# A decoder trunk's first modulation: four parts of 256 features in place of two of 512, with products of two k blocks between them

## The chip, the cores and the metric

The kernel runs on one core of a Trainium2 chip. The metric is the device time of one execution in microseconds (us); before the change it is 2655.22 us, the median of three runs (2654.45 to 2656.13). The engines are PE (TensorE: matrix products and transposes; its weight loads are shown apart as PEld), DVE (VectorE), ACT (ScalarE), POOL (GpSimd) and SP (SyncE, which only issues DMAs here). Each engine takes its instructions strictly in the order in which the program lists them, and waits on semaphores for what other engines or DMAs have to deliver first.

## The reference

Two layers of a decoder on a sequence of 1024 tokens with 1024 features. Every sub-layer is modulated by a vector `c`: a shift, a scale and a gate, each of 1024 features, computed from `c` by one large matrix. The change touches only the first sub-layer's shift and scale, and the first half of what follows them, the columns of `v` in the gated mixer:

```
def ada_mod(c, w, b):
    m = jax.nn.silu(c) @ w + b
    shift, scale, gate = jnp.split(m, 3, axis=-1)
    return shift[:, None, :], scale[:, None, :], 1.0 + gate[:, None, :]

...
    shift, scale, gate = ada_mod(c, ada_w[i, 0], ada_b[i, 0])
    h = x * (1.0 + scale) + shift
...
    uv = jax.nn.gelu(h @ w_in + b_in)
    u, v = jnp.split(uv, 2, axis=-1)
```

All is float32. The kernel gets that precision from products of reduced-precision pairs: an operand is split into a high part (a cast) and a low part (the remainder), and a product is three matmuls: high by high, high by low, low by high.

## The kernel before

The tokens are eight tiles of 128 rows, the features eight k blocks of 128. The first phase is `mixer_a` (L494). It computes, for the first 512 columns of `v`, `v = h @ w_in`, tile by tile and k block by k block, with one PSUM bank for each tile (`psv`).

What must happen first is the modulation. `silu_c` holds silu(c) as eight columns, one for each k block. `ada_rows` (L595) loads one k block of the matrix, 128 rows by 2 x 512 features (shift and scale; 512 KB, rows of 2 KB). DVE multiplies it by its column and adds it to `adaacc` (L619, L621, L645, L647, one instruction of 1024 elements for each block; below, a *step*). When all eight are in, eight small matmuls with a column of ones (`psa_sum`, L606) sum over the partitions and leave shift and scale as columns; `columns` (L598) adds the bias. This is done twice: `mods_first` (L612) for features 0 to 511 (k blocks 0 to 3 of h), `mods_second` (L637) for features 512 to 1023.

`build_hT` (L235), called through `rows_of` (L546), makes h for some tiles and one k block: PE transposes the tiles of x into a PSUM bank (`pst`, L241), ACT applies scale and shift into `h` (L246) and casts the high part (L250), DVE forms the remainder (L251; `hT` in DVE's rows). `h` has two buffers and so have the PSUM banks that `pst` and `psa` share. `v_sum` (L522) issues the products (three for a tile and k block). `v_high` and `v_low` (L510, L518) split 1024 elements of weights, two k blocks, on ACT and DVE.

The order is written out by hand. `in_turn` (L551) is a generator that runs through a list of (tiles, k block): the h of an item is built two items ahead of its products. Between its stops the code places the other work: `mods_second` hands out turns after its steps 1, 2, 4, 6 and 7. `tc.keep_in_program_order` pins an instruction to its place in the order of its engine. While the first modulation is being loaded, PE runs matmuls on ready data without use of the result (`warm_up`, L587): 8 and 13, and 4 more later. All loads are issued on SP's one queue, in the order of the code, and at most eight are under way at a time: the ninth waits for the first to land.

Of the kernel before, what the change touches and what calls it, by code (L numbers as in the profile page):

```python
# [35 lines left out]
def trunk(ctx: ExitStack, tc: tile.TileContext, x, c, ada_w, ada_b, ln_g, ln_b, a_w_in, a_b_in,  # L36
# [83 lines left out]
    def ada_steps(j, order, raw_bufs=2):  # L120
# [4 lines left out]
        for part, h in order:  # L125
# [3 lines left out]
            def step(k, part=part, h=h, box=box, w0=w0):  # L129
                nm = f"{j}_{part}_{h}"  # L130
                raw = ada_p.tile([P, HALF], F32, name=f"adaw_{nm}_{k}", tag="adaw", bufs=raw_bufs)
                nc.sync.dma_start(raw[:], ada_w[i, s, k * P : (k + 1) * P, w0 : w0 + HALF])
                if k == 0:
                    acc = box["acc"] = ada_p.tile([P, HALF], F32, name=f"adaacc_{nm}", tag=f"adaacc{part % 2}")
                    ins = V.tensor_scalar(acc[:], raw[:], silu_c[:, 0:1], None, ALU.mult)
                else:
                    acc = box["acc"]
                    ins = V.scalar_tensor_tensor(acc[:], raw[:], silu_c[:, k : k + 1], acc[:], ALU.mult, ALU.add)  # L138
                tc.keep_in_program_order(ins)
# [354 lines left out]
    def mixer_a():  # L494
        nonlocal ada_p, vec
        with ExitStack() as ph:
# [13 lines left out]
            def v_high(c, kp):  # L510
                raw = vz[:, kp, :] if kp > 1 else wts.tile([P, D], F32, name=f"winv_{c}_{kp}_raw", tag="raw", bufs=2)[:]
                src = a_w_in[0, 2 * kp * P : 2 * (kp + 1) * P, D + c * HALF : D + (c + 1) * HALF]
                nc.sync.dma_start(raw.rearrange("p (k n) -> p k n", n=HALF), src.rearrange("(k p) n -> p k n", p=P))
                hi, lo = units[c, kp] = tuple(wts.tile([P, D], F32R, name=f"winv_{c}_{kp}_{m}", tag=f"w{m}")[:] for m in ("hi", "lo"))
                tc.keep_in_program_order(A.copy(hi, raw))
                parts_of[c, kp] = lo, raw, hi

            def v_low(c, kp):  # L518
                lo, raw, hi = parts_of.pop((c, kp))
                tc.keep_in_program_order(V.tensor_tensor(lo, raw, hi, op=ALU.subtract))  # L520
# [16 lines left out]
            def v_act(c, i):  # L537
                z = vz[:, i, c * HALF : (c + 1) * HALF]
                A.activation(z, z, AF.Gelu_apprx_tanh)
                V.bn_stats(st_v[:, i, c, :], z)  # L540
# [10 lines left out]
            def in_turn(*runs, begin=False):  # L551

                todo = [(i0, n, k) for i0, n, ks in runs for k in ks]
# [6 lines left out]
                for m in range(2):  # L560
                    rows(m)
                    yield
                for m, (i0, n, k) in enumerate(todo):
                    parts = [(i0, TERMS)]
                    if begin and m < 2:
                        parts = [[(0, TERMS[:1]), (0, TERMS[2:])], [(2, TERMS[:1]), (0, TERMS[1:2]), (2, TERMS[2:]), (2, TERMS[1:2])]][m]
                    for i1, terms in parts:
                        for i in range(i1, i1 + n):
                            v_sum(0, i, k, begin, terms)
# [3 lines left out]
            def x_cols(h, tiles):  # L573
                w = slice(h * HALF, (h + 1) * HALF)
                for i in tiles:
                    nc.sync.dma_start(xs[i][:, w], x_in[i * P : (i + 1) * P, w])

            first_ks, last_ks = range(KD // 2), range(KD // 2, KD)
            with tc.tile_pool(name="ada0", bufs=2, reuse_waits="tile") as ada0:
                warm = hT[1][0][:, KD - 1, :]  # L580
                acc = vec.tile([P, 2, HALF], F32, name="adaacc", tag="gate")
# [11 lines left out]
                xs += [work.tile([P, D], F32, name=f"x0_{i}", tag="res", bufs=3) for i in range(4, 7)]  # L593

                def ada_rows(h, k, raw):  # L595
                    nc.sync.dma_start(raw, ada_w[0, 0, k * P : (k + 1) * P, 0 : 2 * D].rearrange("p (t n) -> p t n", t=2)[:, :, h * HALF : (h + 1) * HALF])

                def columns(h, p):  # L598
                    for part in (1, 0):
                        src = p[:, 8 * part : 8 * part + 8].rearrange("p (k t) -> p k t", t=2)[:, :, 0]  # L600
                        bias = cols_b[:, 8 * part + 4 * h : 8 * part + 4 * h + 4]
                        res = ada[0][("add", "mul")[part], h] = cst.tile([P, 4], F32, name=f"ada_0_{part}_{h}")
                        ins = V.scalar_tensor_tensor(res[:], src, float(part), bias, ALU.add, ALU.add)
                        tc.keep_in_program_order(ins)

                def psa_sum(p, part, src, col):  # L606
                    for q in range(4):
                        tc.keep_in_program_order(T.matmul(
                            p[:, 8 * part + 2 * q : 8 * part + 2 * q + 1], src[:, part, q * P : (q + 1) * P], col,
                            start=True, stop=True))  # L610

                def mods_first():  # L612
                    p = bank("tr", "psa_0")
                    for k in range(KD):
                        raw = vz[:, k, :].rearrange("p (t n) -> p t n", t=2)
                        ada_rows(0, k, raw)
                        col = silu_c[:, k : k + 1]
                        if k == 0:
                            V.tensor_scalar(acc[:], raw, col, None, ALU.mult)  # L619
                        elif k < KD - 1:  # L620
                            tc.keep_in_program_order(V.scalar_tensor_tensor(acc[:], raw, col, acc[:], ALU.mult, ALU.add))  # L621
                        else:
                            for part in (1, 0):
                                tc.keep_in_program_order(V.scalar_tensor_tensor(acc[:, part, :], raw[:, part, :], col, acc[:, part, :], ALU.mult, ALU.add))
                        if k == 2:
                            tc.keep_in_program_order(A.copy(warm, raw[:, 0, :]))
                            warm_up(8)
                            pt = bank("tr", "rows_bt")
                            tc.keep_in_program_order(T.transpose(pt[:, 0:P], rows_b[:], ident[:]))
                            warm_up(13)  # L630
                        elif k == 5:
                            tc.keep_in_program_order(V.tensor_copy(cols_b, pt[:, 0:64]))
                    for part in (1, 0):
                        psa_sum(p, part, acc, one[:])
                    columns(0, p)

                def mods_second(between):  # L637
                    for k in range(KD):
                        if k < 6:
                            raw = ada0.tile([P, 2, HALF], F32, name=f"adaw_0_1_{k}", tag="adaw", bufs=6)[:]  # L640
                        else:
                            raw = vz[:, k - 6, :].rearrange("p (t n) -> p t n", t=2)
                        ada_rows(1, k, raw)
                        if k == 0:
                            ins = V.tensor_scalar(acc[:], raw, silu_c[:, 0:1], None, ALU.mult)  # L645
                        else:
                            ins = V.scalar_tensor_tensor(acc[:], raw, silu_c[:, k : k + 1], acc[:], ALU.mult, ALU.add)  # L647
                        tc.keep_in_program_order(ins)
                        for f in between.get(k, ()):
                            f()  # L650
                    p = bank("tr", "psa_1")
                    for part in (1, 0):
                        psa_sum(p, part, acc, one[:])
                    columns(1, p)
# [3 lines left out]
                mods_first()  # L658
                v_high(0, 0)
                x_cols(0, range(4))  # L660
                turns = in_turn((0, 2, (0,)), (2, 2, (0,)), (0, 2, (1,)), (2, 2, (1,)), (0, 4, (2, 3)), (4, 2, first_ks), begin=True)
                v_low(0, 0)
                next(turns)
                warm_up(4)
                next(turns)
                next(turns)
                next(turns)
                v_high(0, 1)
                v_low(0, 1)
                x_cols(0, (4, 5))  # L670
                next(turns)
                mods_second({k: [lambda: next(turns)] for k in (1, 2, 4, 6, 7)})
                x_cols(1, range(4))
                v_high(0, 2)
                next(turns)
                v_low(0, 2)
                rest = in_turn((0, 4, last_ks), (4, 2, last_ks), (6, 2, range(KD)))
                next(rest)
                run(turns)
                v_high(0, 3)  # L680
                v_low(0, 3)
                x_cols(1, (4, 5))
                nc.sync.dma_start(vbias[:], a_b_in[0, D : 2 * D].partition_broadcast(P))
# [1396 lines left out]
```

## Time and profile before

| What | us |
|---|---|
| median of three runs | 2655.22 |
| the profiled execution | 2655.62 |
| its span, from the first instruction to the last | 2653.9 |
| ACT in 40 to 60 us | 14.23 busy of 20 |
| DVE in 40 to 60 us | 11.60 busy of 20 |
| PE in 40 to 60 us | 19.98 busy of 20 |
| PE in 80 to 100 us | 19.64 busy of 20 |

An engine's busy time is the time during which it executes something; waits and DMA issues are not in it. Where an engine is busy all of the time, its own work sets the pace; where another has gaps, the question is whether anyone waits for it. Times in rows of the timeline are microseconds from the start of the span.

### The profile page before, as it was taken

The page shows a single profiled execution, that of the slowest core. Times are in us where ns is not written, and L with a number is a line of the kernel's source. Part 1 is how long each engine was busy: PE and PEld are TensorE (multiplying, and loading weights), DVE is VectorE, ACT ScalarE, POOL GpSimd, SP SyncE. Part 2 cuts the span into 40 slices and gives each one's busy share as a digit, 9 for nine tenths or more (in the row PEclk, how much of TensorE's full clock was granted, in tenths as well). Part 3 has the DMA queues.
Part 4 walks back from the last instruction along what each step waited for, and adds up shares of the span by engine and source line. Part 5 has one row for each costly group of instructions (what it writes and reads, how often), then busy time and mean ns, then how long its engine had stood idle before and what let it go on. Part 6 is the DMA issues. An engine that isn't in the chain of part 4 may idle for free.

```text
span 2653.9 us, 36921 instructions
## 1 busy us (share of the span) xinstructions
PE 2631.0 (99%) x13144; PEld 2179.2 (82%) x13144; DVE 1979.9 (75%) x3558; ACT 1397.1 (53%) x2639; POOL 104.8 (4%) x190
## 2 busy tenths in 40 slices
PE   8999999999999999999999999999999999999998
PEld 6888888888888888888888888888888888888887
DVE  6886898886988787655557777777669965677887
ACT  5454475555444554333436666666657655554432
POOL 0000000000000001111110000000010000000000
PEclk9999999999999999999999999999999999999999
DMA  8543367778867546565565554555783654495562
GB/s 298 187 120 119 127 199 237 240 233 287 315 212 248 186 151 230 192 205 195 175 188 159 151 148 129 141 143 144 233 222 120 211 186 152 151 320 190 180 208 86
DMA packets 341554, 505.35 MB, mean 190 GB/s; under 512 B 58092, under 2 KB 175444, under 8 KB 341368
## 3 DMA queue, kind: packets, MB, share of 16 engines
q1 hardware_dynamic: 324936, 444.22, 53.2%
q0 software_dynamic: 16432, 58.76, 6.2%
q8 instruction: 103, 1.69, 0.3%
q14 instruction: 83, 0.68, 0.1%
HBM read 365.95 MB, written 136.95 MB: 189 GB/s over the span
## 4 chain that ended last, share of the span: by engine, by line
PE 70%; issue 21%; DVE 4%; POOL 2%; DMA 1%; ACT 1%; POOLq 0%; SPq 0%; DVEq 0%; ACTq 0%
PE psua L987 13%; PE psd L1154 12%; PE psk L1600 7%; PE psuc L987 7%; PE psq L1600 6%; PE psd_wout L432 3%; PE psub L987 3%; PE psv L528 3%; PE pv L1773 3%; PE psu L774 3%; PE sc L1693 3%; PE pT L1746 1%; POOL v L1475 1%; PE psoa L1977 1%; POOL qk L1470 1%
## 5 line engine op out<-in xcount | busy, mean ns | idle before, releaser
L987 PE MATMUL psua<-right,left 128*128 128x512 f32 x1536 | 362.9, 390 | 0.1
L1154 PE MATMUL psd<-rhi,lhi 128*128 128x512 f32 x880 | 343.3, 390 | 0.0
L1154 PE MATMUL psd<-rhi,llo 128*128 128x512 f32 x880 | 342.5, 389 | 0.0
L1154 PE MATMUL psd<-rlo,lhi 128*128 128x512 f32 x880 | 342.4, 389 | 0.0
L987 PEld LDWEIGHTS psua<-right,left 128*128 128x128 f32 x1536 | 287.4, 188 | 61.1 <-DVE left L112 0.7
L1715 ACT ACTIVATE p<-p,stat 128x128 f32<-128x128 f32 (+1 forms) x384 | 168.7, 441 | 95.4 <-DVE stat L1713 93.4
L1154 PEld LDWEIGHTS psd<-rhi,lhi 128*128 128x128 f32 x880 | 165.3, 188 | 34.8 <-ACT part L1018 0.9
L1154 PEld LDWEIGHTS psd<-rhi,llo 128*128 128x128 f32 x880 | 165.3, 188 | 34.2
L1154 PEld LDWEIGHTS psd<-rlo,lhi 128*128 128x128 f32 x880 | 165.3, 188 | 33.8
L987 PE MATMUL psuc<-right,left 128*128 128x512 f32 x768 | 186.5, 390 | 0.0
L987 PEld LDWEIGHTS psuc<-right,left 128*128 128x128 f32 x768 | 143.8, 188 | 30.2 <-DVE right L112 0.6
L112 DVE TENSOR_TENSOR pTlo<-pT,pThi 128x512 fp32r<-128x512 f32 (+1 forms) x160 | 99.3, 621 | 76.1 <-ACT pThi L111 75.0
L112 DVE TENSOR_TENSOR left<-ws,left 128x512 fp32r<-128x512 f32 x128 | 88.0, 689 | 81.9 <-ACT left L111 80.1
L112 DVE TENSOR_TENSOR llo<-lraw,lhi 128x1024 fp32r<-128x1024 f32 x112 | 136.2, 1218 | 2.3 <-ACT lhi L111 2.3
L1600 PE MATMUL psk<-form_L,wqk_hi 128*128 128x512 f32 x384 | 127.3, 413 | 1.0 <-DVE qlo L112 1.0
L1600 PE MATMUL psq<-form_L,wqk_hi 128*128 128x512 f32 x384 | 126.7, 411 | 0.0
L111 ACT CAST lhi<-lraw 128x1024 fp32r<-128x1024 f32 x112 | 117.0, 1047 | 11.6 <-PE psd L1154 6.7
L1498 PE MATMUL psv<-vrhi,form_S 128*128 128x512 f32 x384 | 120.0, 391 | 1.4 <-DVE vpart L1464 0.9
L111 ACT CAST left<-ws 128x512 fp32r<-128x512 f32 x128 | 79.2, 620 | 80.0 <-DVE ws L911 69.4
L111 ACT CAST pThi<-pT 128x512 fp32r<-128x512 f32 (+1 forms) x160 | 84.7, 530 | 61.8 <-PE pT L1746 44.9
L1713 DVE CUSTOM_DVE_ANT_0 p<-sc,bias 128x128 f32<-128x128 f32 (+1 forms) x384 | 113.5, 345 | 4.5 <-PE sc L1693 3.3
L138 DVE SCALAR_TENSOR_TENSOR adaacc<-adaw,silu_c,adaacc 128x512 f32<-128x512 f32 x140 | 104.5, 747 | 6.6 <-DMA adaw<-in_ada_w_dram 5.6
(369 smaller groups left out, 6079.8 us busy)
## 6 DMA issues: line engine op xcount, KB each, us to landing
lraw<-forms SPq DMA_DIRECT2D x112, 512.0 KB
adaw<-in_ada_w_dram SPq DMA_DIRECT2D x160, 256.0 KB
up<-in_mlp_w_up_dram SPq DMA_DIRECT2D x64, 512.0 KB
forms<-s SPq DMA_DIRECT2D x128, 256.0 KB
rraw<-in_mlp_w_down_dram SPq DMA_DIRECT2D x64, 512.0 KB
forms<-part SPq DMA_DIRECT2D x96, 256.0 KB
v<-vs POOLq DMA_DIRECT2D x48, 512.0 KB, 3.6
vraw<-in_b_w_qkv_dram SPq DMA_DIRECT2D x42, 512.0 KB
```

The lines of the kernel that those rows point to most:

```text
L111: first = A.copy(hi, src) if hi_engine is A else hi_engine.tensor_copy(hi, src)
L112: return first, lo_engine.tensor_tensor(lo, src, hi, op=ALU.subtract)
L138: ins = V.scalar_tensor_tensor(acc[:], raw[:], silu_c[:, k : k + 1], acc[:], ALU.mult, ALU.add)
L432: T.matmul(p[:], stat[a][:, k, o : o + P], u[b][:, w], start=n == 0, stop=n == count - 1)
L528: ins = T.matmul(sums[i][:], hT[half][a_][:, k, o : o + P], units[c, k // 2][b_][:, n : n + HALF], start=k + a_ + b_ == 0, stop=k == KD - ...
L774: T.matmul(p[:], wu[a_][:, k * P : (k + 1) * P], hT[half][b_][:, k, :], start=k + a_ + b_ == 0, stop=k == KD - 1 and a_ == 1)
L987: T.matmul(acc, w[:, a, k, :], right[p][:, b, k, :], start=p in (1, 2, 5) and k + a + b == 0, stop=k == 3 and a == 1, skip_group_check=True)
L1154: ins = T.matmul(sums[kind, m][:, w], l[a][:, k, m * P : (m + 1) * P], r[b][:, k, w], start=p in (1, 5, 2, 3) and kp + k + a + b == 0 or b ...
L1498: T.matmul(acc, rows[:, m * P : (m + 1) * P], cols_, start=p in (1, 2, 5) and kp + k + a + b == 0, stop=kp == 1 and k == 1 and a == 1, ski ...
L1600: T.matmul(p[:], wu[a][:, k * P : (k + 1) * P], h_op(k, half, b), start=k + c_ == 0, stop=k == KD - 1 and c_ == 2)
L1713: V.tensor_tensor_reduce(out=pr, in0=banks[e][:, sl], in1=st["bias"][:, width - w :], scale=-0.125, scalar=3e38, op0=ALU.add, op1=ALU.min, ...
L1715: A.activation(pr, pr, AF.Exp, bias=nm, scale=-1.0, accum_out=l)
```

## The change

The first sub-layer's modulation is computed in four parts of 256 features (a part gives two k blocks of h) in place of two of 512. A load is 128 rows by 2 x 256 features (256 KB, rows of 1 KB), and a step has 512 elements. Part 0's first product is made by ACT into a tile of its own (`adaacc_a`), and the small matmuls add it to the rest. `adaacc` has two halves, used in turn. After part 0, the products of k blocks 0 and 1 for tiles 0 to 5 run; after part 1 those of k blocks 2 and 3, and so on (`quarter`, `middle`). The weights of `v` are split in halves, one k block at a time, and the first one is loaded in halves too. The tiles' order within a k block is changed, as is the order in which finished sums are taken out (`v_add`, `v_act`). There are 8 + 1 + 4 warming matmuls in place of 8 + 13 + 4. All of these loads are pinned in SP's order, and so are the weights of the gate that is computed later.

```diff
+            def v_high(kp, n):
+                w = slice(n * HALF, (n + 1) * HALF)
+                tc.keep_in_program_order(A.copy(units[0, kp][0][:, w], parts_of[kp][:, w]))
...
+                def mods_step(u, k):
+                    a, raw, col = acc[:, u % 2], raws.pop((u, k)), silu_c[:, k : k + 1]
+                    if k == (u == 0):
+                        ins = V.tensor_scalar(a, raw, col, None, ALU.mult)
+                    else:
+                        ins = V.scalar_tensor_tensor(a, raw, col, a, ALU.mult, ALU.add)
+                    tc.keep_in_program_order(ins)
...
+                def mods_end(u):
+                    p = bank("tr", f"psa_{u}")
+                    psa_sum(p, acc[:, u % 2])
+                    columns(u, p)
...
+                first = in_turn([(0, 2, 0), (2, 2, 0), (0, 2, 1), (2, 2, 1), (4, 2, 0), (4, 2, 1)], begun=TERMS[1:2])
...
+                mods_step(1, 0)
...
+                next(first)
+                mods_step(1, 1)
+                mods_step(1, 2)
+                next(first)
+                for k in (3, 4, 5):
+                    mods_step(1, k)
+                next(first)
+                mods_step(1, 6)
+                mods_step(1, 7)
+                v_high(1, 0)
+                mods_end(1)
+
+                def quarter(u, last):
+                    turns = in_turn([(i0, n, k) for k in (2 * u, 2 * u + 1) for i0, n in ((4, 2), (0, 4))], late=(0,))
+                    next(turns)
+                    v_high(u, 1)
+                    v_low(u, 0)
+                    for _ in last:
+                        pass
+                    next(turns)
+                    v_low(u, 1)
+                    next(turns)
+                    return turns
...
+                def middle(u, turns):
+                    next(turns)
+                    mods_step(u, 0)
+                    mods_step(u, 1)
+                    next(turns)
+                    for k in range(2, KD):
+                        mods_step(u, k)
+                    v_high(u, 0)
+                    mods_end(u)
+
+                middle(2, second)
+                third = quarter(2, second)
...
+                middle(3, third)
...
+                fourth = quarter(3, third)
-                mods_second({k: [lambda: next(turns)] for k in (1, 2, 4, 6, 7)})
```

How this stands on the engines is shown by the order of their instructions. A row gives the line, the operation, out<-in by the program's names and the shape. `adaacc` is the running sum, `psa` its small matmuls, `pst_0_3` the transposes of tiles 0 to 3 (`pst_4_...`: tiles 4 and 5) for k block 3, `h_0_3` the same after scale and shift, `hT_0_1` and `hT_1_1` the remainders of tiles 0 to 3 and of tiles 4 to 7.

DVE before, from the second modulation's fourth step to the columns that it gives:

```order
L647 SCALAR_TENSOR_TENSOR adaacc<-adaw_1_3_330,silu_c,adaacc 128x1024
L647 SCALAR_TENSOR_TENSOR adaacc<-adaw_1_4_333,silu_c,adaacc 128x1024
L251 TENSOR_TENSOR hT_1_1_139<-h_4_0_339,hT_1_0_138 128x256
L647 SCALAR_TENSOR_TENSOR adaacc<-adaw_1_5_355,silu_c,adaacc 128x1024
L647 SCALAR_TENSOR_TENSOR adaacc<-vz,silu_c,adaacc 128x1024
L251 TENSOR_TENSOR hT_1_1_139<-h_4_1_363,hT_1_0_138 128x256
L647 SCALAR_TENSOR_TENSOR adaacc<-vz,silu_c,adaacc 128x1024
L251 TENSOR_TENSOR hT_1_1_139<-h_4_2_380,hT_1_0_138 128x256
L603 SCALAR_TENSOR_TENSOR ada_1_1_399<-psa_390,cols_c 128x4
L603 SCALAR_TENSOR_TENSOR ada_0_1_401<-psa_390,cols_c 128x4
L251 TENSOR_TENSOR hT_1_1_139<-h_4_3_414,hT_1_0_138 128x256
```

DVE now, at the place of the third part of the four:

```order
L253 TENSOR_TENSOR hT_1_1_139<-h_4_3_396,hT_1_0_138 128x256
L625 TENSOR_SCALAR adaacc<-adaw_2_0_274,silu_c 128x512
L627 SCALAR_TENSOR_TENSOR adaacc<-adaw_2_0_274,silu_c,adaacc 128x512
L253 TENSOR_TENSOR hT_0_1_137<-h_0_3_419,hT_0_0_136 128x512
L627 SCALAR_TENSOR_TENSOR adaacc<-adaw_2_2_277,silu_c,adaacc 128x512 x2
L627 SCALAR_TENSOR_TENSOR adaacc<-adaw_2_4_280,silu_c,adaacc 128x512 x2
L627 SCALAR_TENSOR_TENSOR adaacc<-adaw_2_6_283,silu_c,adaacc 128x512 x2
L643 SCALAR_TENSOR_TENSOR ada_1_1_160<-psa_436,cols_c 128x2
L643 SCALAR_TENSOR_TENSOR ada_0_1_159<-psa_436,cols_c 128x2
L253 TENSOR_TENSOR hT_1_1_139<-h_4_4_446,hT_1_0_138 128x256
```

Before, one or two steps of 1024 stood between two remainders; now two steps of 512 stand before the remainder of `h_0_3`, and six behind it, with the columns of the part right after them.

PE before, around the second modulation's small matmuls:

```order
L528 MATMUL psv_4_367<-winv_0_hi,hT_1_0_138 128x512
L528 MATMUL psv_4_367<-winv_0_lo,hT_1_0_138 128x512
L528 MATMUL psv_4_367<-winv_0_hi,hT_1_1_139 128x512
L528 MATMUL psv_5_371<-winv_0_hi,hT_1_0_138 128x512
L528 MATMUL psv_5_371<-winv_0_lo,hT_1_0_138 128x512
L528 MATMUL psv_5_371<-winv_0_hi,hT_1_1_139 128x512
L608 MATMUL psa_390<-one,adaacc 128x1 x8
L241 MATMUL pst_4_3_411<-ident,x_4_153 128x128
L241 MATMUL pst_4_3_411<-ident,x_5_154 128x128
L528 MATMUL psv_4_367<-winv_1_hi,hT_1_0_138 128x512
L528 MATMUL psv_4_367<-winv_1_lo,hT_1_0_138 128x512
```

PE now, around the third part's:

```order
L243 MATMUL pst_0_3_414<-ident,x_0_150 128x128
L243 MATMUL pst_0_3_414<-ident,x_1_151 128x128
L243 MATMUL pst_0_3_414<-ident,x_2_152 128x128
L243 MATMUL pst_0_3_414<-ident,x_3_153 128x128
L538 MATMUL psv_4_327<-winv_1_hi,hT_1_0_138 128x512
L538 MATMUL psv_4_327<-winv_1_lo,hT_1_0_138 128x512
L538 MATMUL psv_4_327<-winv_1_hi,hT_1_1_139 128x512
L538 MATMUL psv_5_331<-winv_1_hi,hT_1_0_138 128x512
L538 MATMUL psv_5_331<-winv_1_lo,hT_1_0_138 128x512
L538 MATMUL psv_5_331<-winv_1_hi,hT_1_1_139 128x512
L633 MATMUL psa_436<-one,adaacc 128x1 x4
L243 MATMUL pst_4_4_443<-ident,x_4_154 128x128
```

Before, the small matmuls came after the products of tiles 4 and 5 for a k block, once; now they come so for each part, and here the four transposes whose remainder stands ahead of six steps on DVE are just six products earlier on PE.

DVE at the start of the program, before:

```order
L619 TENSOR_SCALAR adaacc<-vz,silu_c 128x1024
L621 SCALAR_TENSOR_TENSOR adaacc<-vz,silu_c,adaacc 128x1024 x5
L632 COPY cols_c<-rows_bt 128x64
L621 SCALAR_TENSOR_TENSOR adaacc<-vz,silu_c,adaacc 128x1024
L624 SCALAR_TENSOR_TENSOR adaacc<-vz,silu_c,adaacc 128x512 x2
L603 SCALAR_TENSOR_TENSOR ada_1_0_209<-psa_158,cols_c 128x4
L603 SCALAR_TENSOR_TENSOR ada_0_0_211<-psa_158,cols_c 128x4
L520 TENSOR_TENSOR winv_0_lo<-winv_0_raw,winv_0_hi 128x1024
L251 TENSOR_TENSOR hT_0_1_137<-h_0_0_226,hT_0_0_136 128x256
```

And now:

```order
L625 TENSOR_SCALAR adaacc<-vz,silu_c 128x512
L627 SCALAR_TENSOR_TENSOR adaacc<-vz,silu_c,adaacc 128x512 x4
L672 COPY cols_c<-rows_bt 128x64
L627 SCALAR_TENSOR_TENSOR adaacc<-vz,silu_c,adaacc 128x512 x2
L643 SCALAR_TENSOR_TENSOR ada_1_0_158<-psa_194,cols_c 128x2
L643 SCALAR_TENSOR_TENSOR ada_0_0_157<-psa_194,cols_c 128x2
L253 TENSOR_TENSOR hT_0_1_137<-h_0_0_230,hT_0_0_136 128x256
L530 TENSOR_TENSOR winv_0_lo<-winv_0_raw,winv_0_hi 128x512
L253 TENSOR_TENSOR hT_0_1_137<-h_2_0_248,hT_0_0_136 128x256
```

The first sum is one tensor_scalar and six steps of half the width, as its first block is ACT's; the weights' remainder (`winv_0_lo`) is made in halves, behind the first remainder of h.

243 lines of the change are left out of this document (127 added, 116 removed).

## The prediction

> **What bounds the kernel now.** I read the page's totals first, then windows over the first 80 us, where all of the change lies, then the timeline of that stretch engine by engine.
>
> ```profile
> PE 2631.0 (99%) x13144; PEld 2179.2 (82%) x13144; DVE 1979.9 (75%) x3558; ACT 1397.1 (53%) x2639; POOL 104.8 (4%) x190
> 0.00:10.00 10.00, 0.45 (x1) 0.18 (x1) 3.42 (x12) 1.89 (x3) 1.52 (x7) 1.00 0.76 236
> 10.00:20.00 10.00, 9.73 (x44) 8.00 (x44) 8.41 (x11) 1.72 (x3) 0.00 (x0) 1.00 1.05 393
> 20.00:40.00 20.00, 19.93 (x104) 15.75 (x103) 15.25 (x21) 11.22 (x21) 0.00 (x0) 1.00 1.05 386
> 60.00:80.00 20.00, 20.00 (x102) 15.66 (x101) 18.07 (x31) 14.46 (x27) 1.26 (x2) 1.00 0.69 210
> ```
>
> The first row is the page's; the others give, for each stretch, its length and then PE, PEld, DVE, ACT and POOL busy, the granted clock, the DMA share and GB/s. PE is the bound: 99% of the span, and 20.00 of 20 us at 60 to 80. So a microsecond that PE loses or wins early is carried to the end; an engine beside it costs only where PE waits for it. PE has no real work in the first 20 us: what it does there is warming. DMA is full (393 and 386 GB/s) until 40 us.
>
> ```profile
> 8.40 6.61 DVE L621 SCALAR_TENSOR_TENSOR adaacc<-vz,silu_c,adaacc 128x1024 f32<-128x1024 f32 x5 [1.99 <-DMA vz<-in_ada_w_dram]
> 10.27 3.78 PE L589 MATMUL warm<-hT,ones_r 128*128 128x512 f32 x8 [5.29 <-ACT hT L626]
> 14.77 2.70 PE L589 MATMUL warm<-hT,ones_r 128*128 128x512 f32 x11
> 14.92 0.22 DVE L632 COPY cols_c<-rows_bt 128x64 f32<-128x64 f32 x1
> 16.43 1.41 DVE L624 SCALAR_TENSOR_TENSOR adaacc<-vz,silu_c,adaacc 128x512 f32<-128x512 f32 x2
> 17.31 1.87 PE L608 MATMUL psa<-one,adaacc 128*128 128x1 f32 x16
> 20.60 0.73 PE L528 MATMUL psv<-winv_hi,hT 128*128 128x512 f32 x2
> ```
>
> These are rows of the timeline (start, duration). The second block of the first modulation arrives at 8.40, then DVE takes blocks at 6.61 / 5 = 1.32 us, which is DMA's pace (512 KB at 393 GB/s are 1.33 us). The sum is complete at 16.43 + 1.41 = 17.84, and the first product of the layer starts at 20.60, which is 2.76 us later. The second modulation, on the same engines, hardly holds PE up:
>
> ```profile
> 35.73 1.28 DVE L647 SCALAR_TENSOR_TENSOR adaacc<-vz,silu_c,adaacc 128x1024 f32<-128x1024 f32 x1
> 37.16 1.92 PE L608 MATMUL psa<-one,adaacc 128*128 128x1 f32 x16
> PEld psv L528 <- DVE hT L251: 1.8, 6, 0.5
> PEld psa L608 <- issue: 0.4, 1, 0.4
> ```
>
> Its last step ends at 37.01 and psa runs at 37.16; the last two rows, from the waits between 20 and 120 us, are all that PE loses there to DVE (total, times, longest). The steps were spread between 25.64 and 37, while PE had eight k blocks' worth of other products.
>
> **The change, part by part. 1, the start.** Blocks are half as large. The second now lands about one 1.33 us pace earlier, at 7.1; from there DVE has a tensor_scalar, six steps and the bias copy of 0.22. Prices of the narrow forms:
>
> ```profile
> L135 DVE TENSOR_SCALAR adaacc<-adaw,silu_c 128x512 f32<-128x512 f32 x1 | 0.5, 481 | 0.0
> 65.64 1.53 DVE L138 SCALAR_TENSOR_TENSOR adaacc<-adaw,silu_c,adaacc 128x512 f32<-128x512 f32 x2
> L251 DVE TENSOR_TENSOR hT<-h,hT 128x256 fp32r<-128x256 f32 x11 | 4.6, 420 | 3.2 <-ACT hT L250 3.2
> L251 DVE TENSOR_TENSOR hT<-h,hT 128x512 fp32r<-128x512 f32 x6 | 4.1, 690 | 5.2 <-ACT hT L250 5.1
> ```
>
> A step of 512 elements that follows another costs 1.53 / 2 = 0.765 us, so a block dealt out in two halves costs DVE 1.53 where it cost 1.32. The chain ends at 7.1 + 0.48 + 6 x 0.765 + 0.22 = 12.4. DMA's pace for it, 0.67 a block, puts the last block at 11.1, so DVE ends last. From the full sum to the first product it was 2.76; now seven of eight psa products (0.234 each by 1.87 / 8) come behind the last step, 1.64 us, where 1.34 came before (17.31 + 1.87 - 17.84), so 3.1. First product at 15.5: **-5.1 us**. Bounds: were the rows of 1 KB as slow as the whole blocks of before, the last would land at 16.4, as now, and the gain be about 0; were DVE not last, 11.1 + 0.75 + 3.1 gives 15.0 and -5.6. I take -5.0, nearest to the DVE chain. The x tiles and the half weight follow on the same queue: 0.26 + 0.52 MB behind the last block, 2.0 us, so 13.1, before they are wanted.
>
> **2, the second part's steps.** Between the first hT remainder and psa_1 DVE has six remainders of 256 (0.42 each), two of half a weight (0.69 or a little less), one tensor_scalar and seven steps: 2.5 + 1.3 + 0.5 + 5.4 = 9.7 us, plus waits for ACT, of which the 256 row shows 3.2 us over 11, so some 1.5 for five or six. PE's work in that time is five groups of two transposes and six products:
>
> ```profile
> 52.26 0.38 PE L241 MATMUL pst<-ident,x 128*128 128x128 f32 x2
> 55.23 0.38 PE L241 MATMUL pst<-ident,x 128*128 128x128 f32 x2
> 56.84 0.38 PE L241 MATMUL pst<-ident,x 128*128 128x128 f32 x2
> ```
>
> From 55.23 to 56.84 it is 1.61 a group (the stretch ahead of it, with twelve products, is 2.97). Five are 8.05. PE stands before psa_1 for 11.2 - 8.05 = **+3.1 us**; 1.6 if DVE never waits, 4.5 if it waits twice as long.
>
> **3, the third and fourth parts' steps.** This is the largest term. By the order of DVE, six of the eight steps stand behind the remainder of tiles 0 to 3 for the odd k block (h_0_3, then h_0_5), and that remainder comes only after PE's four transposes of it. On PE there are six products between these transposes and psa. The same passage in the old trace:
>
> ```profile
> 25.45 0.60 PE L241 MATMUL pst<-ident,x 128*128 128x128 f32 x4
> 26.09 0.78 ACT L246 ACTIVATE h<-pst,ada,ada 128x512 f32<-128x512 f32 x1 [0.82 <-PE pst L241]
> 26.90 0.62 ACT L250 CAST hT<-h 128x512 fp32r<-128x512 f32 x1
> 27.27 0.60 PE L241 MATMUL pst<-ident,x 128*128 128x128 f32 x4
> 27.63 0.69 DVE L251 TENSOR_TENSOR hT<-h,hT 128x512 fp32r<-128x512 f32 x1
> 28.23 1.28 DVE L647 SCALAR_TENSOR_TENSOR adaacc<-adaw,silu_c,adaacc 128x1024 f32<-128x1024 f32 x1
> ```
>
> From the transposes (25.45) to the step behind the remainder (28.23) are 2.78 us; six steps add 4.6; psa can start 7.4 us after the transposes. PE gets through the transposes and six products in 27.27 - 25.45 = 1.82. It stands 5.6 us, once before psa_2 and once before psa_3: **+11.2 us**. What is queued behind: the transposes of the next k block, on which ACT waits, and twelve products that need nothing of psa. The blocks themselves are there: up to the third part's last block the queue carries 9.4 MB, 24 us at 390 GB/s from about 5.6, so 30 us, and DVE comes to them at 35. Before, one step stood between two remainders; that is the difference. Bounds: 5.2 each if steps follow one another at 0.69, 6.0 if ACT is late by a cast.
>
> **4, the rest.** psa: three times four products at 0.234 against 1.92 once: **+0.9**. Casts by halves: ACT has 11.22 of 20 us busy, and the remainders by halves lie in DVE's idle time before and after the steps, except those counted in 2; without this cover they would cost 0.1 to 0.2 each, eight times. Twelve warming products fewer: PE is idle there. Later stages: the order differs in places up to the output projection, the work is the same, and PE is full there, so nothing is given back; bound 0 to -1 for waits that a rested DVE spares.
>
> **5, PE after a long wait.** After 5.29 us of idling, PE ran slowly: ten warming products from 10.27 to 14.77, 0.45 each, then eleven in 2.70, 0.25. 4.5 us at 0.45 instead of 0.233 are about 2 us lost. The two waits of 5.6 are as long as that one; the trace does not say whether idling alone does it. 0 to +4; I take **+2**, one of the two. [...]
>
> **Sum:** -5.0 + 3.1 + 11.2 + 0.9 + 2 = **+12.2 us**. The profiled execution took 2655.6 us (span 2653.9 and 1.7 around it), 0.4 above the median of 2655.2, so 2667.8.
>
> **Rivals.** *The early start is kept* (not slower): were the steps done in DVE's idle time, so that PE meets each psa with its sum ready as at 37.16, only -5.0 + 0.9 remain, 2651.5; with a start at its bound, 2650. It needs the 4.6 us of steps off the path from the transposes to psa; for it speaks that DVE is busy only 15.25 of 20 us, against it that the order leaves the steps behind the remainder, and DVE takes its rows in turn. It decides as soon as fewer than two steps stand there (1.5 us of PE's six products hide no more). *Half the stall*: h_0_3 comes earlier than I think because PE is held by something else, or later stages give back: +4 to +8, about 2661. *PE is slow after both waits, and at the first products too*: +15 to +18, about 2672; for it speaks that only nine warming products are left ahead of the sum. *The first part does not come earlier* (the change does not do what it says): DMA is full, and rows of 1 KB could cost what 2 KB cost; then term 1 is 0 and the time 2673. [...]
>
> **How the numbers follow.** Forecast 55 in 100 (own range 2663 to 2670), slow PE 20, half the stall 10, no early start 6, early start kept 9. The range must take in the slow PE (2672 and some) and half the stall down to 2659: 2659 to 2674. About 0.2% (5.3 us) is what a measurement of this kernel can tell from no change. Slower by more: 87 (six of half the stall among them); within: 8 (four of half the stall, four of the kept start); faster: 5.
>
> **What would show it.** In the changed profile: the first psv at 15.5 to 16; an idle time of PE or PEld before psa, released by DVE adaacc, three times, about 3, 5.6 and 5.6 us; steps in a row of six with 0.77 between starts; psv at 0.43 to 0.45 each for some 4 us behind a wait if term 5 holds. Wrong would be: psa without a wait, a first product after 18, or a wait that DMA ends.

## The result and the profile after

The changed kernel takes 2682.44 us (median of 5 runs, 2678.95 to 2683.13) against 2655.22 (2654.45 to 2656.13): 1.0098 times as long, with a 95% interval of 1.0084 to 1.0113. It is slower by 27 us, and the prediction (2667.8, range 2659 to 2674) is too low. The profiled execution took 2678.95 us and its span 2677.2, so the two traces differ by 23.3 us in the span; it is the fastest of the five runs.

The page's totals show that no engine got much more to do (PE had 2631.0 before, DVE 1979.9, ACT 1397.1):

```profile
PE 2640.3 (99%) x13140; PEld 2183.5 (82%) x13140; DVE 1982.7 (74%) x3580; ACT 1398.3 (52%) x2644; POOL 105.5 (4%) x190
```

The waits of PE between its first product and 120 us (total, times, longest) show where the time went; DVE's running sum ends nearly all of it, and no transfer ends any:

```profile
PE psa L633 <- DVE adaacc L627: 13.9, 3, 5.5
PE psv L538 <- ACT winv_hi L111: 1.1, 1, 1.1
PE psa L161 <- ACT adahi L111: 0.6, 1, 0.6
PE psv L538 <- DVE hT L253: 0.5, 1, 0.5
PE psv L538 <- ACT hT L252: 0.4, 1, 0.4
```

The timeline of the third part's passage (start, duration) is the one that the prediction worked out from the old trace:

```profile
36.74 0.60 PE L243 MATMUL pst<-ident,x 128*128 128x128 f32 x4
38.34 0.40 PE L538 MATMUL psv<-winv_hi,hT 128*128 128x512 f32 x1
38.84 0.69 DVE L253 TENSOR_TENSOR hT<-h,hT 128x512 fp32r<-128x512 f32 x1 [2.04 <-ACT hT L252]
39.45 4.68 DVE L627 SCALAR_TENSOR_TENSOR adaacc<-adaw,silu_c,adaacc 128x512 f32<-128x512 f32 x6
44.28 1.84 PE L633 MATMUL psa<-one,adaacc 128*128 128x1 f32 x8 [5.54 <-DVE adaacc L627]
46.88 0.63 PE L538 MATMUL psv<-winv_lo,hT 128*128 128x512 f32 x1
47.30 1.05 PE L538 MATMUL psv<-winv_hi,hT 128*128 128x512 f32 x2
```

From the transposes (36.74) to psa (44.28) it is 7.54 us; 7.4 was predicted. Six steps follow the remainder without a gap. But psa then takes 1.84 us, where the same eight matmuls ahead of the second k blocks took 1.02 (27.80 in the timeline), and products follow one another at 0.42 (46.88, 47.30) instead of 0.23 (50.68, 50.91 in the timeline, at a clock of 1.00). Stretches cut at the waits, with PE, PEld, DVE, ACT and POOL busy, granted clock, DMA share and GB/s:

```profile
26.00:30.10 4.10, 2.30 (x15) 2.11 (x16) 1.85 (x5) 0.89 (x3) 0.00 (x0) 1.00 1.10 353
30.10:33.50 3.40, 3.40 (x12) 2.71 (x11) 1.49 (x3) 2.00 (x4) 0.00 (x0) 0.51 1.07 387
33.50:38.50 5.00, 5.00 (x26) 3.96 (x24) 2.41 (x5) 2.06 (x4) 0.00 (x0) 0.99 1.09 350
38.50:43.80 5.30, 0.24 (x2) 0.00 (x0) 4.78 (x7) 0.83 (x2) 0.00 (x0) 1.00 1.04 360
43.80:50.60 6.80, 6.32 (x20) 5.47 (x21) 1.59 (x5) 1.49 (x3) 0.00 (x0) 0.50 0.49 169
50.60:58.30 7.70, 7.70 (x37) 5.63 (x36) 2.78 (x5) 3.60 (x6) 0.00 (x0) 1.00 0.00 0
60.90:71.10 10.20, 7.16 (x22) 6.05 (x23) 4.04 (x8) 1.49 (x3) 0.00 (x0) 0.50 0.15 53
```

The clock is halved at each of the three waits, for 3.4, 6.8 and 10.2 us (0.51, 0.50 and 0.50 in the rows); of the last 10.2 us, 3.1 lie within the wait itself, which ends with psa at 63.94. In the rows with halved clock PE is busy for 3.40 + 6.32 + 7.16 us at half speed, so half of their sum, 8.4 us, is lost to the clock (an estimate: that the same work would take half as long at full clock). Note the row from 50.60: nothing moves on the load queues any more (0 GB/s), so the fourth part's blocks are in, and DVE is busy for 2.78 of 7.70 us; yet six of the steps run only later, behind the late remainder. The late steps hold up the load queue too: SP waits for 19.0 us for DVE's `adaacc`, and issues no load between 44.8 and 65.8 us. PE does not wait for these loads.

The account, from the trace alone: the first product starts 4.9 us earlier (15.70 against 20.60), the waits take 13.9, the clock 8.4, psa 1.1 more (3 x 1.02 against 1.92). That makes 18.5; at 122 us PE stands 21.6 us later, so 3.1 are left. The small waits in the rows above (2.6, of which the kernel before has 0.4 too) and the half clock on the first products (about 0.4) make up most of them. Behind 122 us another 2.3 are lost; at the end it is 23.9.

### The profile page after: what moved, and what is told of

Read it like the earlier page. It is cut to its first block, busy times and chain, and to the rows that moved or that the text cites. A ratio compares the mean times of both kernels' runs of the same rounds, so it can differ in the third digit from the quotient of the medians.

```text
span 2677.2 us, 36969 instructions
## 1 busy us (share of the span) xinstructions
PE 2640.3 (99%) x13140; PEld 2183.5 (82%) x13140; DVE 1982.7 (74%) x3580; ACT 1398.3 (52%) x2644; POOL 105.5 (4%) x190
## 4 chain that ended last, share of the span: by engine, by line
PE 89%; DVE 5%; DMA 3%; ACT 2%; issue 1%; POOL 0%; SPq 0%; DVEq 0%; ACTq 0%; POOLq 0%
PE psd L1223 21%; PE psua L1056 13%; PE psv L1567 13%; PE psk L1669 7%; PE psuc L1056 7%; PE psq L1669 6%; PE psd_wout L434 3%; PE psub L1056 3%; PE pv L1842 3%; PE sc L1762 3%; PE psu L843 2%; PE psv L538 2%; PE pT L1815 1%; DMA adaw<-in_ada_w_dram 1%; PE psoa L2046 1%
```

## The experiments

Added warming products go into a bank that is overwritten. Starts of the first product of some tiles on PE, read from each trace, serve as landmarks (psv: the first columns of `v`; rows_t: a transpose near their end; psu: `u`; psd_wout: the mixer's output projection; psd_end: the last products). One of them, rows_t, stands six products and two transposes (about 1.6 us) later in PE's order in the changed kernels than in before and the three held kernels, so there only kernels of the same kind are compared without a correction:

```
kernel        median us            psv   rows_t   psu    psd_wout  psd_end
before        2655.2               20.6   62.1   122.5    227.7    2643.8
after         2682.4               15.7   83.8   144.1    250.4    2667.7
warm          2678.6               15.0   84.3   144.6    251.0    2667.0
tick          2679.7               15.0   85.3   145.7    250.8    2669.5
fill          2670.5               15.0   76.3   136.6    243.0    2659.0
one_wait      2671.9               15.8   75.3   135.6    242.5    2659.8
spread        2660.8               15.7   65.6   125.9    232.1    2650.0
spread_warm   2659.5               15.8   64.7   125.0    231.5    2647.2
deal          2657.3               15.4   62.6   121.8    230.3    2646.8
deal_tick     2655.6               15.5   62.7   121.8    226.9    2643.7
deal2_tick    2654.5               15.8   62.4   121.7    227.0    2643.8
held          2662.5               20.2   70.0   130.4    235.6    2650.6
held_fill     2662.1               20.6   68.6   129.1    234.2    2649.9
held_fill2    2661.5               20.3   67.0   127.5    232.6    2649.3
```

### spread: the steps placed earlier

```diff
                     v_low(u, 0)
+                    part_steps(u + 1, 0, 3)
...
                     v_low(u, 1)
+                    part_steps(u + 1, 3, 5)
...
                     next(turns)
-                    mods_step(u, 0)
-                    mods_step(u, 1)
+                    part_steps(u, 5, 8)
                     next(turns)
-                    for k in range(2, KD):
-                        mods_step(u, k)
```

> The steps of the second, third and fourth part are dealt out earlier on DVE (second: 2, 2, 2, 2 over the first four turns; third and fourth: 3, 2 and 3, all ahead of or just behind the remainders that PE waits for), so that none is queued behind the late remainder when psa comes. Nothing else differs from the kernel after (2682 us). Theory 1 (the loss is the three waits before psa and the halved clock behind them): the waits before psa fall from 2.8, 5.5 and 5.5 us to under 1 each, the clock stays at 1.0 from 17 us on, and the time falls by 20 to 26 us, to 2656 to 2662. Rival A (the loss lies elsewhere, in late loads or in the smaller pieces): the waits fall but others take their place, and the time stays above 2670. Rival B (the waits count, the clock does not): -14, about 2668.

Measured: 2660.75 us (2658.72 to 2662.2), 21.7 less than after, and 17.7 by the last products of the two traces (the profiled run of after is its fastest); 1.0022 times before (1.0013 to 1.0031). Same work, loads and pieces; only the steps' places differ, those of the second part too. The waits between 16 and 120 us:

```profile
PE psv L538 <- DVE hT L253: 1.2, 2, 0.7
PE psv L538 <- ACT winv_hi L111: 1.1, 1, 1.1
PE psa L633 <- DVE adaacc L627: 1.0, 3, 0.3
```

13.9 us became 1.0. Rival A (late loads, small pieces) falls: those are unchanged here. Rival B, 2668, falls as well: more went than the waits. One detail of the expectation was wrong: in this run the clock was halved from 12.7 to 19.5 (0.50 in 13.00 to 16.40), over the first products.

### fill and one_wait: the clock apart from the waits

```diff
                     p = bank("tr", f"psa_{u}")
+                    for _ in range({1: 10, 2: 24, 3: 24}[u]):
+                        tc.keep_in_program_order(T.matmul(p[:], ones_r[:], warm, start=True, stop=True))
```

> Warming products (10, 24 and 24, into the bank that psa then overwrites) are put on PE ahead of psa_1, psa_2 and psa_3, where PE idles in the kernel after; the steps of DVE stay as they are. Theory 1 (about 14 us of waiting, and 8 to 9 us more of halved clock): psa starts as late as before or up to 0.5 us later, the clock stays at 1.0 behind each wait, and the time falls by 6 to 9 us, to about 2673 to 2676. Rival B (the clock costs nothing that the end sees): the same time as after, 2679 to 2684, or slower by what the products overshoot.

Measured: 2670.53 us (2670.19 to 2672.08), 11.9 less than after, where 6 to 9 were expected. DVE's rows are as late as in after; PE only computes something useless meanwhile. Stretches of fill around the second wait:

```profile
30.10:38.00 7.90, 7.90 (x39) 6.07 (x39) 4.08 (x8) 4.72 (x9) 0.00 (x0) 1.00 1.08 365
38.00:44.00 6.00, 6.00 (x32) 4.79 (x30) 4.85 (x7) 0.22 (x1) 0.00 (x0) 1.00 1.06 361
44.00:51.00 7.00, 7.00 (x35) 5.38 (x35) 3.15 (x8) 3.87 (x7) 0.00 (x0) 1.00 0.41 149
```

The clock stays at 1.00, and from 44 to 51 PE does 35 instructions where after did 20 in 6.8 us. Rival B (the clock costs nothing that the end sees) falls. By the landmark rows_t the gain is 7.5 us, near the 8.4 of the account, though 0.7 of it is there at the first product already, ahead of the edit; by the last products it is 8.7. By medians it is more, since the profiled run of after is its fastest.

one_wait deals out the fourth part's steps alone and leaves the other two waits:

```diff
-                    mods_step(u, 0)
-                    mods_step(u, 1)
+                    for k in range(2) if u == 2 else range(5, KD):
+                        mods_step(u, k)
```

> The kernel after with the fourth part's steps alone dealt out as in the kernel spread; the second and third part's stay. Theory 1: the wait before psa_3 falls from 5.5 us to under 1 and the three windows of half clock behind it go, the other two waits stay: 7 to 10 us faster than after, 2672 to 2675. Rival B: 5 us faster, 2677.

Measured: 2671.92 us (2670.35 to 2674.32), 10.5 less than after, and 8.5 by rows_t. The waits before psa fall by 5.2 us (from 13.9 to 8.7), and the third stretch of half clock, in which 3.6 us were lost (half of 7.16), goes (1.00 from 60 to 71): 8.8 in all; the waits alone would be 5.2. The first two halved stretches are still there (0.51 from 43.80 to 50.70).

### warm: the first products

```diff
-                warm_up(1)
+                warm_up(8)
```

> Eight warming products in place of one ahead of the first sums, so that PE has less idle time between 11 and 15 us. Theory 1: the halved clock at 13 to 16.5 us goes, the first twelve products take 0.22 in place of 0.4 us: -1 to -2 us against the kernel after. Rival (the first sums wait behind the warming products, which run at half clock themselves): first product 0.5 to 1 us later, no gain or slower by 1.

Measured: 2678.64 us (2677.77 to 2679.32), 3.8 less than after by medians. The mechanism is there: from 13 to 16.4 us the clock is 1.00 (0.50 in after), and the first product starts at 15.0. Its size stays open: the runs of after spread over 4.2 us, and at rows_t this profiled run is 0.4 later than after's; there the clock was halved for 6.8 us behind the first wait, not 3.4. spread_warm has both edits:

> Both edits, the dealt-out steps and the eight warming products. If the two act apart: the time of the first minus 1 to 2 us, 2655 to 2660, which is about the time of the kernel before (2655.2). If the early start of 4.9 us were kept whole with no wait left, 2651.

Measured: 2659.47 us (2658.39 to 2661.2), 1.3 less than spread; 1.0015 times before (1.0006 to 1.0025). The clock is never halved behind the first product (1.00 in each stretch from 15 to 80 us), and no wait before the three psa exceeds 0.3, yet the 4.8 us of the early start are gone by rows_t (64.7, or 63.1 without the 1.6 us of work that before has behind it, against 62.1). The waits behind the first product are 4.5 us in this trace and 0.4 in before's.

### held: the same stall in the kernel before

To see whether the stall needs the four parts at all, four steps of the old second half (1024 elements) were moved behind the last remainder ahead of `psa_1`:

```diff
-                mods_second({k: [lambda: next(turns)] for k in (1, 2, 4, 6, 7)})
+                mods_second({k: [lambda: next(turns)] for k in (0, 1, 2)} | {3: [lambda: next(turns)] * 2})
```

> The kernel before, with its 512-feature halves and 512 KB loads, in which four of the second half's eight steps (4 x 1.3 us) are moved behind the last remainder ahead of psa_1; the work is the same. Theory 1 (steps queued behind a late remainder make PE wait, and a long wait halves the clock behind it, whatever the size of the pieces): one wait of 4 to 5.5 us ahead of psa_1, half clock for one or two windows of 3.4 us behind it, and 2661 to 2664. Rival B (a wait costs only itself): 2659.5 to 2660.5 for the same wait. Rival A (it is the small pieces that cost): about 2655, as before.

Measured: 2662.47 us (2661.67 to 2664.49), 1.0028 times before (1.0018 to 1.0038). Its timeline, and a row of its stretches behind the wait:

```profile
36.34 0.43 DVE L251 TENSOR_TENSOR hT<-h,hT 128x256 fp32r<-128x256 f32 x1 [1.19 <-ACT hT L250]
36.69 2.60 DVE L647 SCALAR_TENSOR_TENSOR adaacc<-adaw,silu_c,adaacc 128x1024 f32<-128x1024 f32 x2
39.32 2.61 DVE L647 SCALAR_TENSOR_TENSOR adaacc<-vz,silu_c,adaacc 128x1024 f32<-128x1024 f32 x2
42.07 3.54 PE L608 MATMUL psa<-one,adaacc 128*128 128x1 f32 x16 [5.41 <-DVE adaacc L647]
```

```profile
42.00:48.40 6.40, 6.33 (x24) 5.78 (x25) 1.41 (x4) 0.97 (x2) 0.00 (x0) 0.50 0.42 147
```

The stall of after, wait and halved clock, is made in the kernel before by the order of one engine alone: psa takes 3.54 us where before it took 1.92. held_fill puts 20 warming products into that wait, held_fill2 25:

> The same with 20 warming products in the wait ahead of psa_1, into the bank that psa_1 then overwrites. Theory 1: the wait of the sum stays (psa_1 comes as late), the clock stays at 1.0, and it is 2 to 4 us faster than the same kernel without them. Rival B: no difference, or slower by what the products overshoot.

Measured: 2662.11 us (2660.92 to 2663.23). A miss: 0.4 less than held, where 2 to 4 were expected. Its stretches behind the wait show why:

```profile
41.50:44.90 3.40, 2.61 (x22) 2.52 (x22) 0.97 (x3) 0.35 (x1) 0.00 (x0) 1.00 0.22 76
44.93:48.34 3.41, 3.41 (x12) 2.72 (x11) 1.56 (x2) 1.39 (x4) 0.00 (x0) 0.50 0.86 249
```

The 20 products ended 0.8 us too early, and after that came psa. PE counts as busy for 2.61 of 3.40 us, and all the same the clock is halved in the next 3.41.

> The kernel held with 25 warming products in place of 20 ahead of psa_1. With 20, 0.9 us of idling and the 1.9 us of psa were left in one stretch of 3.4 us, and the clock was halved once behind it. Theory 1 (a stretch with too little work in it halves the clock, an idle one or not): no idling is left, the clock stays at 1.0, and the time is 2659.5 to 2661, 1.5 to 3 us under held (2662.5). Rival B: 2662 as before.

Measured: 2661.48 us (2661.05 to 2663.12), 1.0 less than held, where 1.5 to 3 were expected. The clock stays at 1.0:

```profile
41.50:44.90 3.40, 3.40 (x26) 3.15 (x25) 0.65 (x3) 0.56 (x1) 0.00 (x0) 1.00 0.28 96
44.93:48.34 3.41, 3.41 (x20) 2.55 (x18) 2.25 (x3) 2.55 (x4) 0.00 (x0) 1.00 0.81 261
```

20 instructions in the second row stand against 12 above. At rows_t it is 3.0 us ahead of held (67.0 against 70.0), at the last products 1.3 (2649.3 against 2650.6); the medians show 1.0. So the mechanism is shown here, and its price in whole runs only roughly.

### deal, tick: what is left of the loss

deal carries spread_warm on, by the gaps that its trace still showed:

```diff
+                    if u and k == 0:
+                        ins = A.mul(a, raw, col)
...
                     psa_sum(p, acc[:, u % 2])
+                    for k in range(2) if u < 3 else ():
+                        mods_step(u + 1, k)
                     columns(u, p)
```

> The kernel spread_warm carried on: each later part's first product goes to ACT, three steps of the next part stand in DVE's idle time around the columns of the part before, the second pair's transposes stand ahead of the first products, and the first activation of the layer's end comes two turns earlier. By the gaps that the trace of spread_warm shows (0.5 before each psa, 0.85 before h_0_3's products, 0.5 at 18.3, 0.4 at 20.5, 0.5 at 60.7, 1.1 at 67.9), 3 to 5 us less than spread_warm: 2654.5 to 2656.5, about the time before. Rival: ACT, now later with its own rows, makes new waits of the same sum, and it stays at 2659.

Measured: 2657.26 us (2655.78 to 2661.51), 1.0009 times before (1.0000 to 1.0019); the expected gain was 3 to 5, and 2.2 came. By the landmarks it is 0.7 us ahead of before at 122 us and 2.6 behind at 228. What happens there is another part of the change: the loop over the last turns of the first columns of `v` runs seven times where it ran eight (`n` counts from 0 to 6, and before to 7; the expectation below says six and seven), each turn hands out one background step of later modulations, and so all of these come one place later. The next two kernels add the missing one to after and to deal:

```diff
             assert n == 6, n
+            tick()
```

> The kernel after, with one more background step handed out at the end of the layer's last turns. Its loop over those turns runs six times where that of the kernel before ran seven, so that each background step of the modulations to come, and the products of its sum, stands one place later against the work from 75 us on. Theory (the 2.3 us that the kernel after loses behind 120 us come from there): the waits before psz (0.8) and psd_wout (0.8) go, the shift against before stays at what it was at 122 us, and it is 1.5 to 2.5 us faster than after, about 2680. Rival (those waits are a consequence of the earlier delays): no difference, 2682. Whole runs of after spread over 4 us, so the landmarks of the two traces decide, not the medians.

> The kernel deal with the same one background step. In the trace of deal PE stood 0.8 us earlier than in before at 122 us and 4.1 later at 322 us. Theory: that loss goes for the most part, 2 to 4 us less than deal (2657.3), 2653.5 to 2655.5. Rival: the same time as deal.

Measured: tick 2679.68 us (2678.47 to 2683.3), deal_tick 2655.6 (2654.96 to 2658.8; 1.0003 times before, 0.9995 to 1.0012), 1.7 less than deal, where 2 to 4 were expected. Waits of PE from 120 to 360 us, first in deal and then in deal_tick:

```profile
PE psz L415 <- ACT vhi L111: 0.9, 1, 0.9
PE psd_wout L434 <- DVE acc L440: 0.8, 1, 0.8
PE psz L415 <- DVE vlo L112: 0.7, 1, 0.7
PE psa L161 <- ACT adahi L111: 0.2, 1, 0.2
```

```profile
PE psd_wout L434 <- DVE acc L440: 0.8, 1, 0.8
```

From psu to psd_wout deal loses 108.5 - 105.2 = 3.3 us against before and deal_tick 105.1 - 105.2, nothing; after loses 106.3 - 105.2 = 1.1 and tick 105.1 - 105.2, nothing. So the waits before psz come from the missing step. In deal they are only half of its 3.3 us; the other half is the clock again. Two stretches of deal show it:

```profile
143.46:146.87 3.41, 1.84 (x7) 0.95 (x7) 3.41 (x7) 3.41 (x7) 0.00 (x0) 1.00 0.00 0
147.27:150.69 3.42, 3.42 (x10) 2.66 (x9) 3.42 (x7) 3.25 (x6) 0.00 (x0) 0.50 0.08 1
```

Two waits before psz, of 0.91 and 0.65 us, stand in the first stretch, and in the next one PE is busy throughout at half clock, which costs 1.7 us (half of 3.42, an estimate as above). deal_tick has neither these waits nor the halved clock.

The wait before psd_wout, 0.8, stays in tick and deal_tick against the expectation; before has none there, and its cause is open. And tick's gain is not seen at the end of the traces, which were to decide: behind 122 us tick loses 2.6 us in all against before (25.7 behind at the last products, 23.1 at psu), and after 2.3. Of tick's 2.6, 0.8 is the wait before psd_wout; where the rest goes is open.

> As deal_tick, with the three waits that the trace of deal still shows taken up: one step less ahead of the second half weight's remainder (0.63 at 19.6), the step behind instead of ahead of the columns (0.38 at 27.9), the additions of tiles 4 and 5 one turn later (0.69 at 58.6). If they add up: 1 to 1.7 us less than deal_tick, 2652 to 2654, under the kernel before (2655.2).

Measured: 2654.48 us (2653.45 to 2655.76), 1.1 less than deal_tick and 0.9998 times before (0.9990 to 1.0007). It is the best version, and it cannot be told from the kernel before; the expected 2652 to 2654 was missed by 0.5. The wait of 0.5 at 58 us, which deal and deal_tick have, stayed in its trace. Its first product is 4.8 us earlier than before's; at 122 us 0.8 are left, and at the end none. Between 20 and 60 us PE is busy 19.44 and 19.49 of 20 us, where before had 19.93 and 19.98: that is about 1 us of small waits, and another is psa in three pieces (about 2.9 us in all against 1.92). The other 2 of the 4 us that go until 122 us are not fully explained. DVE has 16.66 of 20 us to do in the first of the two stretches where it had 15.25.

```profile
20.00:40.00 20.00, 19.44 (x101) 14.94 (x101) 16.66 (x31) 11.97 (x23) 0.00 (x0) 1.00 1.09 362
40.00:60.00 20.00, 19.49 (x95) 14.92 (x94) 11.73 (x22) 11.73 (x20) 0.00 (x0) 1.00 0.74 225
```

## Why the prediction was wrong

The direction was right, and so was the mechanism of the waits. The step that failed is the price of the clock (5); the stages that were put at nothing (4) cost something too.

- **1, the start: right in size, in part by luck.** -5.0 predicted, -4.9 measured (15.70 against 20.60). The chain of DVE began at 5.84, not 7.1, and ended at 11.67, not 12.4. From there to the first product it took 4.0 us, not 3.1: the clock was halved from 13.07 to 16.48 (0.50), over the last sums, the transposes and the warming products (in warm, where it was not, the first product starts at 15.0). The two errors nearly cancel.
- **2 and 3, the waits: right.** 3.1, 5.6 and 5.6 predicted; 2.83, 5.54 and 5.54 measured, released by DVE's `adaacc`. In term 2 luck helped: both chains were some 1.2 us longer than reckoned (DVE 12.4 for 11.2, from 15.27 to 27.65; PE 9.3 for 8.05, from 15.70 to 24.97). Term 3 came out in its parts as well: 7.54 us for 7.4 from the transposes to psa. spread and one_wait show that the place of the steps makes them, held that it needs nothing else of the change.
- **4, the rest: wrong in one sentence.** psa cost 1.1 where 0.9 was predicted. But "the order differs in places up to the output projection, the work is the same, and PE is full there, so nothing is given back; bound 0 to -1" failed: 2.3 us were lost behind 122 us, and 3.1 ahead of it, mostly in small waits. PE being full in the old trace meant that the old order fed it, not that any order does; tick and deal_tick show that one background step out of place costs 1.1 (after) and 3.3 us (deal) up to psd_wout; the other 1.2 in after, of which 0.8 is the wait before psd_wout, are not fully explained, and tick does not end with a smaller loss than after.
- **5, PE after a long wait: the step that failed.** +2 was taken, with bounds 0 to +4; it is 8.4 by the account, 7.5 to 8.7 by the landmarks of fill and 11.9 by its medians. Three things were missed. Behind the wait of 2.83 us the clock was halved as well (0.51 from 30.10 to 33.50), and the prediction counted the two long waits only. The slow stretch at a long wait was not some 4.5 us, of which about 2 are lost: it was 6.8 and 10.2 us, two and three times 3.41, in which PE is busy for 6.3 and 7.2 us. And psa itself runs in it, at 1.84 us for 1.02. Taking one wait of the two also halved the term. The rival "PE is slow after both waits" named the mechanism and priced it at 2672, by 4.5 us of slow products behind each wait; 6.3 and 7.2 us of slow work came, and 3.4 behind the shorter wait.

The five terms with their measured sizes, -4.9 + 2.8 + 11.1 + 1.1 + 8.4, make 18.5 where 12.2 was predicted; with the 3.1 and 2.3 that had no term it is 23.9, the last product's delay. That the median lies 3.5 us above the profiled run is the spread of after's five runs, 4.2 us. Whether that is more than before's is not shown: its first runs spread over 1.7 us, but 24 of them, measured with the last kernels, over 4.0. The clock was halved for 3.4 us behind the first wait in the trace of after and for 6.8 in those of warm and tick; whether such differences add to the spread was not measured.

## What to carry to other kernels

Work that was spread over DVE's idle time was free here only at the places where its queue was idle (13.9 us of waits before psa in after, 1.0 in spread, with the same steps): look for what stands behind the last instruction that the bound engine waits for, not at the busy share (DVE is busy for 75% of the span before and 74% after). Waits of the matrix engine of 2.8 to 5.5 us had to be priced here at about one and a half times their length (22.3 us for 13.9 in after; 7.9 by rows_t for 5.4 in held), and products that do nothing, put into the wait, took the second part back where they filled it (7.5 us by rows_t in fill, 3.0 in held_fill2). Two shorter waits close together had a halved clock behind them too: in deal, 0.91 and 0.65 us within one stretch of 3.41 us, and a clock of 0.50 in the next 3.42. When a loop over turns is cut shorter, see what else is handed out in it.

## What the runs showed of the hardware

Up to 76 us the granted clock in the record of after changes at 13.07, 16.48, 30.14, 33.55, 43.79, 50.62, 60.86 and 71.10 us, each a whole multiple of 3.41 us after the one before. I cut all fourteen traces (before, after and the twelve runs) on that grid, each from the first entry of its clock record (9.3 to 14.6 us) to 76 us and 0.4 us ahead of the grid, and added up the columns that PE streamed in each of the 259 stretches: 512 for a product, 128 for a transpose, 1 for a matmul of psa. The fullest stretch of before has 7424 (from 31.3 us) and that of after 7168 (from 19.5 us), both at a clock of 1.00; at 0.50, after has 4096 in a stretch in which PE is busy throughout (46.8 to 50.2).

```
columns in the stretch    stretches    clock in the next 3.41 us
0 to 2560                 32           halved in all 32
2820 and more             227          full in all 227
```

With the cut 0.2 us ahead the two groups stay apart too; with 0 or 0.6 us there are exceptions. Of the 32 stretches in the first row 17 have over 1000 columns. Four of the 32, in each of which PE worked: in after, the stretch with the wait of 2.83 us (2312 columns in 26.3 to 29.7, clock 0.50 in 30.14 to 33.55) and two that another slow one follows (776 in 43.4 to 46.8, 1800 in 63.9 to 67.3, clock 0.50 in 47.20 to 50.62 and in 67.68 to 71.10); and held_fill's with PE busy 2.61 of 3.40 us (784 columns, since most of that time was psa, and 0.50 in 44.93 to 48.34).

The 0.4 us was chosen on these stretches, so the table describes them and predicts nothing. From 76 us to the end of the same traces all 18 stretches with up to 2560 columns are followed by half clock (14 of them are empty ones at the program's end), and all 10577 with more than 3328 by full clock; of the eight between 2688 and 3328, two are followed by half clock, one of them deal's above, with 3072, so there the groups are not apart. What sets the clock is not shown: the counts are of fourteen traces of one kernel and its variants, and no run was made to try them.
